# Moving the stores of an add-and-GELU kernel from SP's DMA queue to ACT's, and their start into the last load

## The chip, the cores and the metric

The kernel runs on one core of a Trainium2 chip. Its engines have short names in the profiles: ACT is ScalarE, DVE is VectorE, POOL is GpSimd, and SP is SyncE, which does no arithmetic here and only issues transfers. Transfers are moved by 16 DMA engines. L87 is line 87 of the kernel's source. The metric is the device time in microseconds (us) of that core. Before the change the median of three runs was 123.27 us (123.16 to 123.56). A profiled execution also has a span, which is a little shorter (121.5 us here), and all times inside a profile count from the start of that span. No matmul is used, and the granted clock was 1.00.

## The reference

Two float32 arrays of 1024 x 4096 are added, and the tanh form of GELU is applied to the sum:

```python
def reference(x, y):
    z = x + y
    return (0.5 * z * (1 + np.tanh(np.sqrt(2 / np.pi) * (z + 0.044715 * z ** 3)))).astype(np.float32)
```

Two inputs of 16.78 MB are read and one output of 16.78 MB is written: 50.33 MB through the DMA engines, whatever the kernel does.

## The kernel before

Each of 128 partitions owns 32768 consecutive numbers. `zt` holds all of x on chip, becomes z in place, and finally holds the result. y has two buffers of 8192 numbers per partition. The work is cut into 32 chunks of 1024 numbers per partition. For each chunk POOL adds (`add`; DVE does it for the first chunk), ACT squares (`sq`), DVE forms the argument (`stt`), ACT takes the sigmoid (`sig`), and DVE multiplies (`mul`).

```python
    loads = [2048, 6144, 8192, 8192, 8192]
    stores = [8192, 8192, 8192, 4096, 4096]
    ...
    def load_y(i):
        ...
        nc.sync.dma_start(out=yt[s][:, o : o + b - a], in_=yv[:, a:b])

    def store(i):
        a, b = sr[i]
        nc.sync.dma_start(out=ov[:, a:b], in_=zt[:, a:b])
    ...
    sp = []
    for i in range(len(loads)):
        sp += [(load_x, i), (load_y, i)]
    sp += [(store, i) for i in range(len(stores))]
    pool = [(add, c) for c in range(C) if c in by_pool]
    dve, acts = [], []
    for i in range(-3, C + 1):
        if 0 <= i < C:
            dve.append((stt, i))
            acts.append((sig, i))
        if 0 <= i - 1 < C:
            dve.append((mul, i - 1))
        ...
        if 0 <= i + 2 < C:
            acts.append((sq, i + 2))
```

So SP's one DMA queue holds ten loads (x0, y0, ..., x4, y4) and then five stores. The last load, y4, reuses a buffer of y and can only be issued when chunk 15 has been added. In DVE's stream `mul` of a chunk stands behind `stt` of the next one; this matters in one experiment.

## Time and profile before

| what | where it is read | value |
|---|---|---|
| time, span | times; page | 123.27 us, 121.5 us |
| DMA engines' share of 16 engines' span | page, queues | 97.2% |
| DVE, POOL, ACT busy | page, part 1 | 62%, 60%, 52% |
| first of the eight adds behind y4 | timeline of POOL | 81.67 us |
| last multiply ends; last store is issued | chain; timeline of SP | 104.8 us |
| last store's first packet | packet records of the trace | 114.5 us |
| last data packet ends | packet records of the trace | 120.2 us |

Lines of the profile page of the kernel before. The digits after DMA are tenths of busy time of the 16 DMA engines in 40 equal slices of the span.

```profile
span 121.5 us, 248 instructions
...
DVE  0035700039999209999996999995999999500000
...
POOL 0028000499990099999969999959999990000000
DMA  3999999998989999999999999899999999999993
...
q1 hardware_dynamic: 2160, 50.33, 97.2%
```

All compute engines have gaps, and in the last five slices they do nothing at all. The DMA row is full from the second slice to the last but one, and there is a single queue, q1.

The windows view of the kernel before (stretch, its length, busy times of DVE, ACT and POOL with counts of instructions, clock, DMA share, GB/s). A packet is counted whole in the stretch in which it starts, so a share can pass 1:

```profile
20.00:42.00 22.00, 13.90 (x12) 11.66 (x12) 13.89 (x6) 1.00 1.02 441
42.00:60.80 18.80, 15.10 (x14) 13.61 (x14) 18.50 (x8) 1.00 1.00 432
...
76.00:80.00 4.00, 4.00 (x4) 3.54 (x4) 4.00 (x2) 1.00 1.06 393
80.00:84.00 4.00, 3.68 (x4) 1.94 (x2) 2.57 (x3) 1.00 0.91 393
84.00:105.00 21.00, 19.71 (x17) 16.55 (x17) 16.18 (x8) 1.00 1.01 435
105.00:118.00 13.00, 0.00 (x0) 0.00 (x0) 0.00 (x0) 1.00 0.99 425
```

The first two rows are loads only, the last two stores only. The rates are nearly the same.

The timelines of SP and of POOL of the kernel before (start, duration, instruction; in brackets how long the engine had been idle, and what ended that):

```profile
60.80 0.33 SPq L77 DMA_DIRECT2D y<-in_y_dram  x1
61.23 43.93 SPq L81 DMA_DIRECT2D out_dram<-z  x5
```

```profile
61.72 18.52 POOL L87 TENSOR_TENSOR z<-z,y 128x1024 f32<-128x1024 f32 x8 [0.94 <-DMA y<-in_y_dram]
81.67 18.52 POOL L87 TENSOR_TENSOR z<-z,y 128x1024 f32<-128x1024 f32 x8 [1.43 <-DMA y<-in_y_dram]
```

The first store is issued right behind y4, the last of the five at 104.8 us. POOL's last eight adds start when y4 has landed, at 81.67 us. The chain that the profile prints ends with the last multiply, so it seems to blame y loads, POOL and DVE:

```profile
DMA y<-in_y_dram 49%; POOL z L87 17%; DVE z L107 8%; DVE w L98 8%; SPq L70 1%; SPq L77 1%; ACT w L92 1%; POOLq L87 0%
```

The chain covers compute up to 104.8 us, and the span goes on for 16.7 us. The last store waits behind the other stores until 114.5 us. Compute is early by 9.7 us.

### The profile page before, as it was taken

To read this page: it belongs to the slowest core of one execution; us is meant where nothing else is said; L and a number is where in the kernel's file an instruction comes from. 1 tells how busy PE (TensorE), PEld (TensorE's weight loads), DVE (VectorE), ACT (ScalarE), POOL (GpSimd) and SP (SyncE) were. 2 spreads that over 40 slices of the span, in tenths; PEclk is the share of its full clock that TensorE was granted. 3 is DMA by queue.
4 is the path that set the end of the run, shared out by engine and by line. 5 is a ranking of instruction groups with operands and counts; after the bars stand their busy time and mean duration, and the time that the engine had idled before them with its cause. 6 is when DMAs were issued, how large, how long until landed. Compare 5 with 4: busy or idle time off the path is not lost.

```text
span 121.5 us, 248 instructions
## 1 busy us (share of the span) xinstructions
DVE 75.5 (62%) x66; ACT 63.8 (52%) x66; POOL 73.0 (60%) x35
## 2 busy tenths in 40 slices
DVE  0035700039999209999996999995999999500000
ACT  4004400068886028788767887883878878100000
POOL 0028000499990099999969999959999990000000
DMA  3999999998989999999999999899999999999993
GB/s 89 421 440 494 413 389 494 391 496 367 496 378 486 389 475 389 475 389 475 389 475 389 475 389 475 345 432 434 424 432 432 442 421 442 421 442 389 426 437 130
DMA packets 2162, 50.35 MB, mean 415 GB/s; under 512 B 240, under 2 KB 240, under 8 KB 240
## 3 DMA queue, kind: packets, MB, share of 16 engines
q1 hardware_dynamic: 2160, 50.33, 97.2%
q14 instruction: 2, 0.02, 0.0%
HBM read 33.55 MB, written 16.78 MB: 414 GB/s over the span
## 4 chain that ended last, share of the span: by engine, by line
DMA 49%; POOL 17%; DVE 16%; SPq 2%; ACT 1%; issue 0%; POOLq 0%
DMA y<-in_y_dram 49%; POOL z L87 17%; DVE z L107 8%; DVE w L98 8%; SPq L70 1%; SPq L77 1%; ACT w L92 1%; POOLq L87 0%
## 5 line engine op out<-in xcount | busy, mean ns | idle before, releaser
L87 POOL TENSOR_TENSOR z<-z,y 128x1024 f32<-128x1024 f32 x31 | 72.8, 2389 | 26.9 <-DMA y<-in_y_dram 26.9
L92 ACT ACTIVATE w<-z 128x1024 f32<-128x1024 f32 x32 | 32.9, 1028 | 38.7 <-POOL z L87 31.4
L98 DVE SCALAR_TENSOR_TENSOR w<-w,z 128x1024 f32<-128x1024 f32 x32 | 39.4, 1232 | 21.1 <-ACT w L92 21.1
L107 DVE TENSOR_TENSOR z<-w,z 128x1024 f32<-128x1024 f32 x32 | 38.8, 1214 | 0.0
L103 ACT ACTIVATE w<-w 128x1024 f32<-128x1024 f32 x32 | 31.4, 981 | 0.4 <-DVE w L98 0.4
L87 DVE TENSOR_TENSOR z<-z,y 128x1024 f32<-128x1024 f32 x1 | 1.2, 1224 | 7.3 <-DMA y<-in_y_dram 7.3
L146 ACT ACT_TABLE_LOAD x1 | 1.3, 1283 | 0.7 <-PEq L172 0.7
L145 DVE MEMSET one<- 128x1 f32 x1 | 0.1, 59 | 0.8 <-PEq L172 0.8
L172 POOL MEMSET const-float32-0.0<- 128x1 f32 x1 | 0.1, 98 | 0.2 <-issue 0.2
L146 ACT ACTIVATE one<-one 128x1 f32<-128x1 f32 x1 | 0.2, 203 | 0.0
L172 POOL MEMSET const-bfloat16-1.0<- 128x1 bf16 x1 | 0.1, 101 | 0.0
L172 POOL MEMSET const-uint8-127<- 128x1 uint8 x1 | 0.1, 101 | 0.0
L172 POOL MEMSET const-float32-1.0<- 128x1 f32 x1 | 0.1, 98 | 0.0
## 6 DMA issues: line engine op xcount, KB each, us to landing
z<-in_x_dram SPq DMA_DIRECT2D x3, 4096.0 KB, 34.2
y<-in_y_dram SPq DMA_DIRECT2D x3, 4096.0 KB, 24.8
out_dram<-z SPq DMA_DIRECT2D x3, 4096.0 KB, 30.3
out_dram<-z SPq DMA_DIRECT2D x2, 2048.0 KB, 17.4
z<-in_x_dram SPq DMA_DIRECT2D x1, 3072.0 KB, 13.8
y<-in_y_dram SPq DMA_DIRECT2D x1, 3072.0 KB, 20.6
z<-in_x_dram SPq DMA_DIRECT2D x1, 1024.0 KB, 4.9
y<-in_y_dram SPq DMA_DIRECT2D x1, 1024.0 KB, 6.9
```

The costliest lines, as they stand in the source:

```text
L70: nc.sync.dma_start(out=zt[:, a:b], in_=xv[:, a:b])
L77: nc.sync.dma_start(out=yt[s][:, o : o + b - a], in_=yv[:, a:b])
L87: eng.tensor_add(out=zt[:, a:b], in0=zt[:, a:b], in1=yt[s][:, o : o + b - a])
L92: nc.scalar.activation(out=wt[c], in_=zt[:, a:b], func=act.Square, scale=root)
L98: nc.vector.scalar_tensor_tensor(out=wt[c], in0=wt[c], scalar=c1, in1=zt[:, a:b], op0=alu.add, op1=alu.mult)
L103: nc.scalar.activation(out=wt[c], in_=wt[c], func=act.Sigmoid)
L107: nc.vector.tensor_mul(out=zt[:, a:b], in0=wt[c], in1=zt[:, a:b])
L145: nc.vector.memset(one, 0.0)
L146: nc.scalar.activation(out=one, in_=one, func=act.Sigmoid)
L172: nc = _bacc.Bacc("TRN2", target_bir_lowering=False, num_devices=1)
```

## The change

The intent is to start storing while the last load is still under way, and to take the stores out of the load queue. The diff:

```diff
     def store(i):
         a, b = sr[i]
-        nc.sync.dma_start(out=ov[:, a:b], in_=zt[:, a:b])
+        nc.scalar.dma_start(out=ov[:, a:b], in_=zt[:, a:b])
...
-    sp += [(store, i) for i in range(len(stores))]
+    behind = {19: [0, 1], 25: [2], 29: [3], C - 1: [4]}
...
         if 0 <= i < C:
             dve.append((stt, i))
             acts.append((sig, i))
+            late = [(store, k) for k in behind.get(i, [])]
+        else:
+            late = []
...
         if 0 <= i + 2 < C:
             acts.append((sq, i + 2))
+        acts += late
```

In ACT's stream stores 0 and 1 now stand behind Square 21, store 2 behind Square 27, store 3 behind Square 31, and store 4 behind the last Sigmoid.

## The prediction

> **What bounds the kernel now.** DMA bytes. The 40-slice view shows the 16 DMA engines at 9 or 10 tenths in every slice but the first and last; the queue view puts 97.2% of 16 engines' span on the one queue, 50.33 MB. DVE (62%), POOL (60%) and ACT (52%) wait for it. The windows view gives 432 to 441 GB/s in the load stretches from 3 to 61 us and 420 to 439 in the store stretch from 85 to 115, so a byte costs about the same in either direction. The chain of waits names POOL and DVE near the end, but stops at 104.8 us, where the last store is issued; the span ends at 121.5 because queued stores have about 16 us left to drain (33.5 MB of loads done at 81.5 us, then 16.8 MB of stores, 40 us at 420 GB/s). So compute has roughly 12 us of slack: the last store (2 MB, about 5 us) is issued that long before the DMA engines reach it.
>
> **What the change does.** No byte and no instruction goes. SP issues ten loads; the stores go to ACT's stream: 0 and 1 after Square 21, 2 after Square 27, 3 after Square 31, 4 after the last Sigmoid.
> - Before, stores 0 and 1 are issued from 61.2 us on, but stand behind the last load on the same queue. Now they are issued at about 76.7 us (Square 21 starts at 75.65) on a second queue, when about 2 MB of the last y load are left. [...] Then the rest of the load takes twice as long: y4 lands at about 85.5 us in place of 81.5.
> - Everything behind slides by 4 us: the last eight adds (2.31 us each on POOL), DVE behind them, the last multiply ending at about 109.
> - Issue cost: 0.33 us each on SP; on ACT there is 0.37 us idle in each 2.31 us chunk. The pair costs perhaps 0.5 us once, absorbed by the wait for the last load.
>
> **How much is on the critical path.** Nearly nothing, as long as the DMA engines never run dry. Estimate: from 76.7 us, 2 MB of loads plus 8.4 MB of stores keep them busy to about 101; store 2, issued at about 96, to 111; store 3, issued at 105.5, to 116; store 4, issued at 109, to 121. Each comes 5 to 7 us early. [...]
>
> **Predicted:** 123.3 us, range 122.3 to 124.6. Faster by over 2%: 0.02; within 2%: 0.94; slower by over 2%: 0.04.
>
> **What would show it.** DMA slices at 9 or 10 throughout; two hardware queues, about 33.6 and 16.8 MB, together near 97%; POOL's last eight adds starting at about 86 us, not 81.7; DVE's last multiply ending at about 109; final landing still near 121.5. Wrong if the slices dip near 101, 111 or 116 us, or if the stretch from 77 to 86 leaves 410 to 450 GB/s.
>
> **What would make it wrong.** Arbitration that favours stores: if y4 waited for all 8.4 MB, compute would end near 124 us and the time near 130. Mixed reads and writes 10% slower over 9 us would cost 1 us; faster ones would gain as much. A final imbalance of engines (0.68 share in the last 6.5 us) that the second queue changes is worth 1 to 2 us at most.

Two sentences are cut out of the forecast, where marked. They were its grounds for taking it that two queues share each DMA engine equally, and that both use the same 16 engines. The 4 us of slip of y4 rest on the assumed equal sharing.

## The result

In the same rounds the changed kernel took 123.56 us (median of 6 runs, 123.46 to 123.76) and the kernel before 123.19 us (6 runs, 123.03 to 123.56). The ratio is 1.0029 with a 95% interval of 1.0013 to 1.0045: the same time, within 2%, with a possible loss of 0.3% that is examined below. Ratios in this document are the mean time of one kernel's fast runs over that of the other's fast runs of the same rounds, so they are not quite the ratio of the medians quoted.

Lines of the profile page after the change:

```profile
span 121.7 us, 244 instructions
...
DVE  0025700039999209999996999995399999910000
...
POOL 0028000499990099999979999934999996000000
DMA  3999989898989899989999999999999998989992
...
q1 hardware_dynamic: 1440, 33.56, 65.1%
q10 hardware_dynamic: 720, 16.78, 32.0%
```

There are two queues now, 65.1% and 32.0%, together 97.1% against 97.2% before. The DMA row is full as before. Only the compute rows moved to the right at their ends.

The same stretches in the windows view after the change:

```profile
76.00:80.00 4.00, 4.00 (x4) 3.58 (x4) 4.00 (x2) 1.00 1.06 393
80.00:84.00 4.00, 3.72 (x4) 1.94 (x2) 0.41 (x2) 1.00 0.91 393
84.00:105.00 21.00, 17.71 (x16) 15.82 (x17) 18.36 (x8) 1.00 1.00 430
105.00:118.00 13.00, 1.99 (x2) 0.73 (x1) 0.00 (x0) 1.00 1.00 430
```

POOL has 2.2 us less work between 80 and 84 us and makes it up later. The bytes moved in those two rows of 4 us are the same in both kernels, although the loads now share them with stores.

The timelines of ACT (its DMA issues) and of POOL after the change:

```profile
75.69 1.03 ACT L92 ACTIVATE w<-z 128x1024 f32<-128x1024 f32 x1 [0.37 <-POOL z L87]
75.70 0.86 ACTq L81 DMA_DIRECT2D out_dram<-z  x2
76.65 0.98 ACT L103 ACTIVATE w<-w 128x1024 f32<-128x1024 f32 x1
...
107.02 0.34 ACTq L81 DMA_DIRECT2D out_dram<-z  x1
```

```profile
61.76 18.51 POOL L87 TENSOR_TENSOR z<-z,y 128x1024 f32<-128x1024 f32 x8 [0.93 <-DMA y<-in_y_dram]
83.86 18.50 POOL L87 TENSOR_TENSOR z<-z,y 128x1024 f32<-128x1024 f32 x8 [3.59 <-DMA y<-in_y_dram]
```

Two things are to be seen. First, ACT's sequencer issued both stores while Square 21 was running, and Sigmoid 20 started at 76.65 us (76.61 before): the issues took nothing from ACT. Second, the adds behind y4 start 2.2 us later than before, and the last multiply and the last store's issue slip with them (104.84 to 107.02 us). That issue still comes 7.5 us before the first packet of the last store, which is at 114.54 us in the records of either kernel (114.545 and 114.537).

What the DMA engines did is plain in the packet records of the trace. A packet is one row of 32 KB or less; each has a start, a duration and a queue. In both kernels the median packet of 32 KB took 1.213 us (loads alone 1.215, stores alone 1.213). That is 32768 B / 1.213 us = 27.0 GB/s per engine. The first store packet of the changed kernel started at 79.52 us, when each of the 16 engines had about one load packet of 32 KB left.

The two profiled runs differ by 0.27 us in span (121.46 and 121.72). The last store's first packet doesn't differ, but the last data packet ends at 120.18 us before and at 120.45 us after. So in this pair the difference arises while the last store drains, on the engine that ends last; the mean over the 16 engines of the time at which they finish (their last semaphore packet) differs by only 0.07 us.

### The profile page after: what moved, and what is told of

The parts are those of the page before. It is cut to its first block, busy times and chain, and to the rows that moved or that the text cites. A ratio compares the mean times of both kernels' runs of the same rounds, so it can differ in the third digit from the quotient of the medians.

```text
span 121.7 us, 244 instructions
## 1 busy us (share of the span) xinstructions
DVE 75.5 (62%) x66; ACT 63.8 (52%) x66; POOL 73.0 (60%) x35
## 3 DMA queue, kind: packets, MB, share of 16 engines
q1 hardware_dynamic: 1440, 33.56, 65.1%
## 4 chain that ended last, share of the span: by engine, by line
DMA 51%; POOL 17%; DVE 16%; SPq 2%; ACT 1%; issue 0%; POOLq 0%
DMA y<-in_y_dram 51%; POOL z L87 17%; DVE z L107 8%; DVE w L98 8%; SPq L70 1%; SPq L77 1%; ACT w L92 1%; POOLq L87 0%
```

## The experiments

The theory is that the DMA engines set the time alone: the same bytes at the same rate, so it doesn't matter which queue they stand in or in what order, as long as the engines never run dry. Compute's slip is paid from a slack of somewhat under 10 us. The rivals were: mixed loads and stores cost real time (rival 1), stores from ACT's queue cost real time at the end (rival 2), and compute is part of the bound.

### The 0.3%: once more, and each half of the change alone

`r1_after_again` is the changed kernel, unedited.

> The changed kernel once more, in 5 rounds. Main theory (the DMA engines set the time, the change costs nothing but scatter of the start-up and of single engines): ratio to before 0.999 to 1.002. Rival 1 (mixed loads and stores cost real time) and rival 2 (stores issued from ACT's queue cost real time at the end): the 1.003 of the first measurement comes back, about 0.35 us.

Measured: 123.49 us against 123.41 us, ratio 1.0010 (0.9993 to 1.0026).

`r2_act01_sp234` moves only the two early stores:

```diff
-        nc.scalar.dma_start(out=ov[:, a:b], in_=zt[:, a:b])
+        eng = nc.scalar if i < 2 else nc.sync
+        eng.dma_start(out=ov[:, a:b], in_=zt[:, a:b])
...
-    behind = {19: [0, 1], 25: [2], 29: [3], C - 1: [4]}
+    sp += [(store, k) for k in (2, 3, 4)]
+    behind = {19: [0, 1]}
```

> Only stores 0 and 1 from ACT while the last load is under way; stores 2, 3, 4 stay on SP. y4 still lands near 83.7 us, the last multiply ends near 107.0. Rival 1 (mixing costs): ratio 1.003. Rival 2 (the tail of stores on ACT's queue costs): ratio 1.000. Main theory: within 0.2% of 1.

Measured: 123.52 us, ratio 1.0005 (0.9988 to 1.0022). The adds behind y4 started at 84.12 us.

`r3_sp01_act234` moves only the three late ones:

```diff
-        nc.scalar.dma_start(out=ov[:, a:b], in_=zt[:, a:b])
+        eng = nc.sync if i < 2 else nc.scalar
+        eng.dma_start(out=ov[:, a:b], in_=zt[:, a:b])
...
-    behind = {19: [0, 1], 25: [2], 29: [3], C - 1: [4]}
+    sp += [(store, k) for k in (0, 1)]
+    behind = {25: [2], 29: [3], C - 1: [4]}
```

> Only stores 2, 3, 4 from ACT; stores 0 and 1 stay on SP behind the last load, so no load shares the DMA engines with a store. y4 lands near 81.5 us again, last multiply near 104.8. Rival 1: ratio 1.000. Rival 2: ratio 1.003. Main theory: within 0.2% of 1.

Measured: 123.35 us, ratio 0.9991 (0.9974 to 1.0008). The adds behind y4 started at 81.55 us.

None of the three is distinguishable from the kernel before, and their intervals end at 1.0026, 1.0022 and 1.0008. Rival 1 expected 1.003 of `r2_act01_sp234` and rival 2 expected 1.003 of `r3_sp01_act234`; both values lie outside the intervals. The loss of 0.3% did not come back in full with the same kernel. A loss of 0.1 to 0.2% can't be excluded by these runs; no claim is made for one.

### The other side of the theory: let the DMA engines run dry

`r4_late01` delays the two stores by three places in ACT's stream, until the last load has landed:

```diff
-    behind = {19: [0, 1], 25: [2], 29: [3], C - 1: [4]}
+    behind = {22: [0, 1], 25: [2], 29: [3], C - 1: [4]}
```

> Stores 0 and 1 from ACT behind Square 24 instead of Square 21, so they can only be issued after y4 has landed and Add 24 is done, at about 84.0 us; first packet near 85.1 against 80.6 before. Main theory: the DMA engines stand idle for 4 to 4.5 us between last load and first store and every idle microsecond is lost: time 127.2 us, 126.5 to 128. y4 near 81.5, last multiply near 104.8 as before. A rival that sees the compute chain as the bound expects no change, since adds and multiplies end where they ended before.

Measured: 126.96 us against 123.41 us, ratio 1.0287 (1.0269 to 1.0304), so 3.55 us slower. The windows view of this run:

```profile
78.00:80.00 2.00, 2.00 (x2) 1.91 (x2) 2.00 (x1) 1.00 0.72 311
80.00:82.00 2.00, 2.00 (x3) 1.73 (x2) 1.11 (x2) 1.00 0.00 0
82.00:84.00 2.00, 1.69 (x2) 0.71 (x2) 2.00 (x2) 1.00 0.02 4
84.00:86.00 2.00, 1.43 (x2) 1.64 (x3) 2.00 (x2) 1.00 1.24 524
```

From the last load packets, which end near 80.5 us, to 84.4 us the engines move practically nothing, 3.85 us in the packet records where 4 to 4.5 were expected, and the time is longer by about as much. In this profile the last multiply ended at 104.3 us, half a microsecond earlier than before the change, and the kernel was still slower. A compute bound can't explain that. The two stores were issued at 83.52 us and the first packet started at 84.39 us, 0.87 us later, with the engines idle.

### How much delay of the last load is free

These two put whole stores ahead of y4 in the single queue of the kernel before. No second queue is involved.

```diff
+    sp.insert(-1, (store, 0))                        # s1_one_ahead; the other four follow y4
+    sp[-1:-1] = [(store, 0), (store, 1)]             # s2_two_ahead; the other three follow y4
```

> All on SP's one queue, store 0 (4 MB) put ahead of the last y load. y4 lands 9.7 us later, near 91.5; last multiply near 114.9 instead of 104.8. Main theory: compute's slack of about 10 us is just used up; the last store is issued as the DMA engines run out of the other stores (about 115.2), its first packet follows about 1 us later: time 124.0 us, 123.3 to 124.8. A rival that says any delay of the last load is paid in full expects 123.2 + 10 = 133 us.

> All on SP's one queue, stores 0 and 1 (8 MB) ahead of the last y load. y4 lands 19.5 us later, near 101.2; last multiply near 124.5. Main theory: past the slack the delay is paid one for one: store 4 starts near 125.6 with the DMA engines idle since about 115, time 133.7 us, 132.5 to 135. If instead slack is larger than I think or delay is hidden, the time stays near 124.

Measured: `s1_one_ahead` 124.25 us against 123.40 us, ratio 1.0075 (1.0045 to 1.0105). `s2_two_ahead` 133.78 us, ratio 1.0846 (1.0805 to 1.0888).

The timeline of POOL in the first and the second of these (last eight adds):

```profile
91.93 18.51 POOL L87 TENSOR_TENSOR z<-z,y 128x1024 f32<-128x1024 f32 x8 [11.52 <-DMA y<-in_y_dram]
```

```profile
101.68 18.52 POOL L87 TENSOR_TENSOR z<-z,y 128x1024 f32<-128x1024 f32 x8 [21.45 <-DMA y<-in_y_dram]
```

A slip of 10.3 us (81.67 to 91.93) cost 0.85 us, and a slip of 20.0 us cost 10.4 us. So the first 9.5 us or so are free and the rest is paid one for one (9.55 us for 9.75 us of slip between the two runs). That is a hinge, and the change's slip of 2.2 us lies far on the free side.

One part of the expectation for `s2_two_ahead` was wrong although the time was right. The windows view of that run:

```profile
100.00:108.00 8.00, 2.89 (x3) 3.58 (x4) 6.32 (x3) 1.00 0.00 0
108.00:114.00 6.00, 6.00 (x6) 4.89 (x6) 6.00 (x4) 1.00 1.02 437
114.00:116.00 2.00, 2.00 (x3) 1.63 (x3) 2.00 (x2) 1.00 1.22 524
116.00:120.00 4.00, 4.00 (x4) 3.50 (x4) 4.00 (x2) 1.00 0.87 369
120.00:125.00 5.00, 4.82 (x5) 2.95 (x3) 0.20 (x1) 1.00 0.54 229
```

I expected the engines to be idle from 115 us. They stood still for 7.2 us right behind y4, from 101.1 to 108.3 us in the packet records, and for 2.5 us more from 123.2 to 125.7, before the last store. The first gap is there because the next store needs `mul` of chunk 23, and that stands in DVE's stream behind `stt` of chunk 24, which waits for y4; that store was issued only at 107.5 us. In total the engines lost about 10 us, and the end is set by the last multiply (124.8 us), so the time came out as expected.

### Mixing much more

`e17_earlier` issues stores 0 and 1 two chunks earlier (`behind = {17: [0, 1], 25: ...}`), so far more of y4 shares the engines with them.

> Stores 0 and 1 two chunks earlier, behind Square 19, issued at about 71.1 us. In the changed kernel their first packet came 3.8 us after the issue, when one load packet of 32 KB per DMA engine was left, and y4 slipped by about two packets of 1.21 us (one store packet ahead of the last load packet, one ahead of its semaphore). Main theory: first store packet near 74.9 us, about 5 load packets left on each engine, slip about 6 packets or 7 us: y4 near 88.5, last multiply near 112, still inside the slack: ratio 1.000, within 0.4%. If the prediction's picture held (first packet 1 us after the issue, half rate from then on), y4 would land near 91 and the last multiply end near 114.5.

Measured: 123.42 us against 123.32 us, ratio 1.0002 (0.9974 to 1.0029). The last line of POOL's timeline:

```profile
88.58 18.52 POOL L87 TENSOR_TENSOR z<-z,y 128x1024 f32<-128x1024 f32 x8 [8.37 <-DMA y<-in_y_dram]
```

A slip of 6.9 us, three times that of the change, cost nothing. The slack was still not used up: the last store was issued at 111.76 us and its first packet started at 114.83 us.

The packet records of this run show the sharing. The stores were issued at 71.00 us; their first packet started at 75.96 us, 4.96 us later, when 4 load packets per engine were left. From then on the engines alternated, one store packet of 1.213 us, one load packet of 1.213 us, with hardly an exception. The expectation had the first packet 1 us too early and five load packets left in place of four. That y4 still came when expected is in part luck: five store packets ahead of the semaphore make 6.1 us of the 6.9, and the last two of its 16 updates came late, at 88.06 and 88.45 us, the others by 87.71. The last load packets ended between 85.6 and 86.3 us, but the first of the 16 small packets (4 bytes each) that follow y4's data and precede the 16 updates of its semaphore, for which POOL waits, started only at 86.85 us: one more store packet came before it. The changed kernel shows the same: most engines ended their last load packet between 80.6 and 81.2 us and sent the semaphore packet near 82, behind one store packet; three engines, which had one store packet before the last load packet too, sent it at 83.2 to 83.4; the last update of the semaphore came at 83.73 us, and POOL's add started at 83.86. The kernel before sent all 16 semaphore packets directly behind the load, between 80.6 and 81.2 us.

### The disputed cost by itself

`p_seq` and `p_mix` have no arithmetic. Their outputs are wrong, which doesn't matter for the times. Everything from the four queues of work to the end of the scheduling loop is replaced:

```diff
+        for i in range(len(loads)):
+            load_x(i)
+            load_y(i)
+        for i in range(len(stores)):
+            store(i)          # p_seq: nc.sync.dma_start; p_mix: nc.scalar.dma_start
```

> No arithmetic at all (the result is wrong on purpose): the same ten loads and five stores of the same sizes on SP's queue, stores behind loads. Main theory: the DMA engines alone set the time of the whole kernel: 122.9 to 123.5 us, at most 0.5% under before. If compute were part of the bound, this would be several us faster.

> As p_seq, but the stores come from ACT's queue, each as soon as the x data that it copies has landed, so loads and stores share the DMA engines for most of the span instead of 4 us. Main theory (a packet takes 1.21 us in either direction, mixed or not): within 0.5% of p_seq. Rival 1 (mixed traffic is slower, by about 0.35 us in 4 us): many us slower, 127 us or more.

Measured: `p_seq` 123.09 us and `p_mix` 123.12 us, beside 123.32 us for the kernel before; ratios 0.9974 (0.9952 to 0.9996) and 0.9976 (0.9955 to 0.9998). The queues of `p_mix`, from its page:

```profile
DMA  4999998999999999999989898989898989989993
...
q1 hardware_dynamic: 1440, 33.56, 65.4%
q10 hardware_dynamic: 720, 16.78, 32.1%
```

Its first store packet started at 19.9 us and its last load packet at 111.5 us, and in between the two directions shared the engines in four stretches (19.9 to 37.8, 46.9 to 64.4, 75.9 to 94.6 and 105.0 to 112.8 us), together about 62 us in place of 4. In the records from 30 to 110 us the 32 KB packets of both queues took 1.213 us on average. Rival 1 is refuted: a mixture costs nothing that these runs resolve. And a kernel with all the transfers and no arithmetic is only 0.2 us faster than the whole kernel. Compute is no part of the bound beyond these 0.2 us.

### An attempt to beat both

The only slices that aren't full are the first and the last. `y0_on_act` issues the first y load from ACT at the same moment as SP issues the first x load; the rest is the kernel before. The cut shows the load alone; the issue was also moved from SP's stream to the start of ACT's.

```diff
-        nc.sync.dma_start(out=yt[s][:, o : o + b - a], in_=yv[:, a:b])
+        eng = nc.scalar if i == 0 else nc.sync
+        eng.dma_start(out=yt[s][:, o : o + b - a], in_=yv[:, a:b])
...
```

> An attempt to beat both: before, with the first y load (1 MB) issued from ACT at the same time as SP issues the first x load, because the only slices that are not full are the first 1.5 us after the first packet and the end. Expected: at best 0.3 to 0.5 us faster (ratio 0.996 to 0.998)[...].

Measured: 123.37 us against 123.32 us, ratio 0.9998 (0.9979 to 1.0016). A miss: no gain. (The expectation also allowed for no change, under a supposed cause of the slow first packets that no run shows; that clause is cut.) The first 8 KB packets of a run took up to 1.198 us in the kernel before and 1.387 us in the changed kernel, where the median of later ones is 0.309 us, and issuing two loads at once didn't change the time. Why the first packets are slow is open. No version that beats both kernels was found, and two orders without arithmetic, `p_seq` and `p_mix`, are only 0.2 us faster. Orders other than those shown in this document were not tried. In the profile before, a DMA engine is busy for 118.1 of 121.5 us on average, so an order that filled every gap, with packets no faster, could give about 3.4 us at most (an estimate). Nearly all of that lies at the two ends of the span: the first packet starts at 1.7 us, and the last one ends 1.3 us before the span does.

## Why the prediction was right

- **The bound.** Predicted: DMA bytes, with compute early. Shown from both sides: without arithmetic the time is 123.09 us, and 3.85 us without DMA traffic cost 3.55 us (`r4_late01`).
- **The time.** Predicted 123.3 us, 122.3 to 124.6; measured 123.56 us in the first comparison and 123.49 us in the second. The DMA row stays full, the two queues add up to 97.1%, and the dips that would have shown a mistake near 101, 111 and 116 us are absent.
- **Arbitration.** That the two queues share the engines equally, packet by packet, was an assumption when the forecast was made. The traces agree with it: with 4 load packets left per engine (`e17_earlier`), load and store packets of 1.213 us alternate one to one, and stores are not favoured. That both queues run on the same 16 engines was assumed too; the runs agree, since the shares of the two queues in the 16 engines' span add up to 97.1% after the change, against 97.2% for the one queue before, and `p_mix` and `p_seq` differ by 0.03 us.
- **A term of wrong size: the slip of y4.** Predicted 81.5 to 85.5 us, measured to 83.7 (adds at 83.86). I took the stores to be issued at 76.7 us and to share from about then on, with 2 MB left to load. They were issued 1 us earlier, at 75.70, but their first packet came only 3.8 us later, with about 16 load packets of 32 KB left, 0.5 MB. On idle engines the same step took 0.87 us in `r4_late01` and 1.00 us for the first load of the kernel before, so about 3 us of the 3.8 came with engines that were busy with loads. In `e17_earlier` it was 4.96 us with loads, and in `r3_sp01_act234` 3.56 us with stores of the other queue. What holds the packet back is not shown. I also had not counted that the semaphore packet of the load would come behind a store packet, as it did here (near 82 us, after load packets that ended between 80.6 and 81.2). One store packet in front of the last load packet or of its semaphore is 1.2 us; on the slowest engines there were two, and that is the 2.2 us slip. The predicted 109 us for the last multiply was too late by 2 us for the same reason.
- **A term of wrong size: the slack.** Predicted roughly 12 us, from the span's end minus 5 us for the last store. Measured 9.7 us from the issue of the last store to its first packet. About 0.9 us of that is not free: so long did it take from issue to first packet even on idle engines (0.87 us in `r4_late01`). The engines don't finish in step (their last packets end at 119.69 us on average in the kernel before, the last of all at 120.19), and the last data packet ends 1.3 us before the span does. The experiments put the hinge near 9.5 us. Nothing hung on it here, because both the predicted slip and the measured one lie far inside either figure.
- **A cost that didn't appear.** I allowed 0.5 us for the pair of issues on ACT. The issues overlapped Square 21 and Sigmoids 20 to 22, the last ones before the wait for y4, started 0.03 to 0.04 us later than before, as the five ahead of the issues also did (0.04 to 0.05).
- **A badly chosen sign.** I wrote that leaving 410 to 450 GB/s between 77 and 86 us would show the prediction wrong. Both kernels moved 401 GB/s there. A round or two of load packets just before the first store packet are slow in either kernel (1.3 to 2.05 us in place of 1.213). It is so in `p_seq` too, which has no arithmetic (up to 2.14 us), but not where stores joined again later in `p_mix`, three times, with no 32 KB packet over 1.213 us, nor in `r4_late01`, where the stores were issued only after the last load had landed (longest 32 KB load packet after 70 us: 1.221 us); why is open. The right test was equality with before, not a fixed band.

What stays open: whether the change costs 0.1 to 0.2%. The first comparison gave 1.0029, the second 1.0010, and neither half alone showed a loss.

## What to carry to other kernels

Here, with the DMA row full from end to end, moving transfers to another queue or another order was worth nothing (ratio 1.0029 and 1.0010), even where it moved compute by 6.9 us (1.0002). In such a kernel look for moments when the engines would run dry, and price those in full: here 3.85 us of them cost 3.55 us. Before pricing a slip of compute, measure how long the last store waits between its issue and its first packet: that is the free slack, and here it was 9.7 us; 6.9 us of slip were free and 10.3 us were not quite. The printed chain of waits can end well before the span does, here at 104.8 of 121.5 us, and then it names work that isn't the bound.
